# A convolution and retention trunk on one core: the rough mean goes into PSUM by ScalarE where the last four tiles begin, and the third weight pair is negated and added earlier

## The chip, the core and the metric
The kernel runs on one core of a Trainium2 chip. A core has five engines, each with a queue of its own that it works through in order: TensorE (PE: matrix products into PSUM), VectorE (DVE), ScalarE (ACT), GpSimd (POOL) and SyncE (SP, which only issues DMAs). PSUM is the small memory that TensorE writes; VectorE and ScalarE read and write it too, GpSimd does not. SBUF is the main memory on the core. The metric is device time in microseconds (us), the median over runs; less is better.

## The reference
Two layers on a sequence of 512 tokens with 1024 features: a causal convolution module and a retention module, each with a norm ahead, a gate and a residual, and one norm at the end. The change touches the first:

```python
def conv_module(h, w_in, dw_w, dw_b, ln_g, ln_b, w_out):
    proj = h @ w_in
    a, b, z = jnp.split(proj, 3, axis=-1)          # 2048 channels each
    u = a * jax.nn.sigmoid(b)
    c = causal depthwise convolution of u, 31 taps, + dw_b
    mu = jnp.mean(cf, axis=-1, keepdims=True)      # over the channels, for each token
    var = jnp.mean(jnp.square(cf - mu), axis=-1, keepdims=True)
    cn = (cf - mu) * lax.rsqrt(var + EPS) * ln_g + ln_b
    y = jax.nn.silu(cn) * jax.nn.silu(z)
    return y @ w_out
```

## The kernel before
Activations lie with channels on the 128 partitions and the 512 tokens along the free axis, so the 2048 channels of the convolution are 16 tiles `c_sb[0..15]` of 128x512. Matrix products run in float32 pieces: every operand is split into a rounded part (`hi`) and a rest (`lo`), and a product is three matmuls (`mm3`, lines 231 to 233): hi x hi, hi x lo, lo x hi.

Weights come from DRAM in 64 pairs of 1 MB (`load`, issued by SP) into two `raw` buffers. Pairs 3 to 23 are split like this: ScalarE writes minus the rounded weights to `lo` (`neg_hi`, line 196), a DMA issued by GpSimd adds `raw` onto it (`dma_lo`, line 204), and ScalarE writes the rounded weights to `hi` (`pos_hi`, line 200). A `raw` buffer is free for the pair after next when both its DMA and its positive copy have ended. Pairs 1 and 2 are split by ScalarE and GpSimd (`split_pair`) while the eight input tiles `h` are made (`h_tile`, `h_lo`).

TensorE works through units of 24 matmuls, two units to a pair; two units give one tile `u` (line 668, with a sigmoid by ScalarE, line 666), and units 32 to 47 give the gate (line 761). Beside that runs the convolution. Tile j is 31 multiplications of a shifted `u` by a column of `cpar`, added up. Two tiles are open at a time. VectorE does most taps (line 515), accumulating in one of two PSUM buffers (`ACC`). Other taps are products by ScalarE (line 434) that GpSimd adds up in SBUF (`accp`, line 442, which is `tadd`, line 297), or pairs of products (line 416) that a DMA issued by GpSimd adds (line 423). For tiles 2 to 11 ScalarE copies the sum of these into the PSUM buffer (`take_up`, line 467) and VectorE goes on from it. Tiles 0, 1 and 12 to 15 are `apart`: VectorE keeps its own sum in PSUM, and one add joins both parts at the end (line 494).

The variance needs the mean. After eight tiles TensorE has a rough mean (matmuls of line 642 and 653), which ScalarE puts into SBUF as `M0` (line 655). Tiles 0 to 11 have it subtracted by GpSimd (`shift`, line 596). In tiles 12 to 15 it is part of VectorE's first tap: `u * w - M0`, line 515 with `M0` as second tensor. Each finished, shifted tile is then summed over the channels by TensorE with a column of ones (`dsum`, line 286), squared by ScalarE (line 610), and the squares are summed, too (`st`). After all 16 sums the mean and variance are known and the layer goes on.

No scheduler orders this stage. The program keeps a clock of its own for each engine (`Clock`, costs written into the code), and at each step `fill` takes the piece of work that by these clocks can start first; what comes out is one fixed order for each engine, recorded as it is written. A change of a condition or of a step's place therefore changes the order of everything after it in this stage. Line numbers in the profile of the changed kernel are higher by up to 10.

## Time and profile before
| | us |
|---|---|
| median of 3 runs (lowest, highest) | 816.16 (814.44, 816.88) |
| the profiled execution | 812.21 |
| its span in the trace | 810.3 |
| TensorE busy | 786.7 (97%) |
| VectorE busy | 587.1 (72%) |
| ScalarE busy | 415.9 (51%) |
| GpSimd busy | 358.7 (44%) |

The busy shares are means over stages: in the convolution stage, from about 34 to 292 us, VectorE and TensorE are busy nearly all the time, and VectorE much less behind it. The profile names an instruction by line, engine and operation; `mm<-g,whi` writes a PSUM tile `mm` from the tiles `g` and `whi`, buffer numbers left out. Convolution tiles and `M0` are all called `g`; `acc` is a PSUM accumulator, `accp` a GpSimd sum, `u` an input of the convolution. What stands in square brackets is the idle time of that engine just before an instruction and what ended it. A timeline merges equal instructions that follow each other: `x5` with the time from the first's start to the last's end.

### The profile page before, as it was taken

Reading aid. Unit: us, or ns where it says so; the run is one execution under the profiler, and the core shown is the slowest. Engines: PE = TensorE matmul, PEld = TensorE weight load, DVE = VectorE, ACT = ScalarE, POOL = GpSimd, SP = SyncE. Lnnn points to the kernel's source line nnn. Section 1 sums busy time; section 2 is a strip of 40 time slices with the busy share of each in tenths; the row PEclk is TensorE's granted clock in tenths of the full one; section 3 lists DMA queues with packets and bytes.
Section 4 is the critical chain, followed back from the end, with each engine's and each line's share of the span. In section 5 each row is a group of like instructions: output and inputs, shape, how many; then the busy total and the mean of one; then the engine's idle time right before and its main releaser. Section 6 shows DMA issues by size and latency. Waiting matters only on the chain.

```text
span 810.3 us, 9659 instructions
## 1 busy us (share of the span) xinstructions
PE 786.7 (97%) x3649; PEld 648.6 (80%) x3650; DVE 587.1 (72%) x862; ACT 415.9 (51%) x550; POOL 358.7 (44%) x280
## 2 busy tenths in 40 slices
PE   7998999999999699999999999999999999999995
PEld 3586878888888587888888888888888888888895
DVE  4997999999999967899664657576586467552434
ACT  4588888878988636632433414414424524331421
POOL 0469999867999758740320223331340121000300
PEclk9999999999999889999999999999999999999999
DMA  7286767999789625422313212112112213323103
GB/s 273 105 208 158 199 169 177 216 217 228 202 195 244 185 47 182 182 97 106 110 53 104 77 79 104 53 53 104 53 53 105 104 53 104 104 91 116 53 1 104
DMA packets 19245, 102.61 MB, mean 127 GB/s; under 512 B 2304, under 2 KB 4352, under 8 KB 8320
## 3 DMA queue, kind: packets, MB, share of 16 engines
q1 hardware_dynamic: 14448, 74.73, 25.8%
q0 software_dynamic: 4320, 26.74, 16.9%
q10 hardware_dynamic: 432, 0.54, 0.2%
q8 instruction: 28, 0.46, 0.2%
q14 instruction: 17, 0.14, 0.1%
HBM read 73.17 MB, written 2.10 MB: 93 GB/s over the span
## 4 chain that ended last, share of the span: by engine, by line
PE 69%; DVE 12%; ACT 6%; POOL 4%; DMA 4%; issue 3%; DVEq 0%; POOLq 0%; ACTq 0%; SPq 0%
PE mm L231 20%; PE mm L232 20%; PE mm L233 20%; DVE acc L515 10%; POOL accp L297 4%; PE mm L958 2%; PE mm L957 2%; PE mm L956 2%; DMA wlo<-raw 1%; ACT wlo L196 1%; ACT whi L200 1%; ACT prod L434 1%; DMA raw<-wpack 1%; PE mm L326 1%; DMA g<-xT 1%
## 5 line engine op out<-in xcount | busy, mean ns | idle before, releaser
L231 PE MATMUL mm<-g,whi 128*128 128x512 f32 (+1 forms) x832 | 321.0, 386 | 0.0
L232 PE MATMUL mm<-g,whi 128*128 128x512 f32 (+1 forms) x832 | 318.5, 383 | 0.0
L233 PE MATMUL mm<-g,wlo 128*128 128x512 f32 (+1 forms) x832 | 317.7, 382 | 0.0
L515 DVE SCALAR_TENSOR_TENSOR acc<-u,cpar,acc 128x512 f32<-128x512 f32 x327 | 222.5, 750 | 6.8 <-ACT acc L467 5.5
L297 POOL TENSOR_TENSOR accp<-accp,prod 128x512 f32<-128x512 f32 x131 | 180.4, 1442 | 12.6 <-ACT prod L434 6.8
L231 PEld LDWEIGHTS mm<-g,whi 128*128 128x128 f32 x832 | 157.2, 189 | 30.9 <-issue 1.2
L232 PEld LDWEIGHTS mm<-g,whi 128*128 128x128 f32 x832 | 157.1, 189 | 30.3 <-issue 1.2
L233 PEld LDWEIGHTS mm<-g,wlo 128*128 128x128 f32 x832 | 157.0, 189 | 30.3 <-DMA wlo<-raw 0.2
L185 ACT CAST whi<-raw 128x1024 fp32r<-128x1024 f32 x80 | 80.6, 1050 | 111.4 <-PE mm L232 69.3
L190 DVE TENSOR_TENSOR wlo<-raw,whi 128x1024 fp32r<-128x1024 f32 x70 | 94.5, 1384 | 41.3 <-ACT whi L185 41.3
L297 POOL TENSOR_TENSOR g<-g,g 128x512 f32<-128x512 f32 x23 | 35.5, 1545 | 179.9 <-ACT g L293 171.4
L434 ACT ACTIVATE prod<-u,cpar 128x512 f32<-128x512 f32 x131 | 90.2, 717 | 24.9 <-POOL accp L297 24.8
L1044 POOL TENSOR_TENSOR g<-g,g 128x512 f32<-128x512 f32 x8 | 10.4, 1295 | 142.7 <-DVE g L1042 142.7
L226 DVE TENSOR_TENSOR g<-g,g 128x512 fp32r<-128x512 f32 x36 | 29.0, 820 | 35.7 <-ACT g L225 32.2
L225 ACT CAST g<-g 128x512 fp32r<-128x512 f32 x36 | 22.4, 621 | 60.1 <-POOL g L1044 27.8
L232 PE MATMUL mm<-wlo,g 128*128 128x512 f32 x128 | 49.8, 389 | 0.0
L233 PE MATMUL mm<-whi,g 128*128 128x512 f32 x128 | 49.6, 389 | 0.0
L231 PE MATMUL mm<-whi,g 128*128 128x512 f32 x128 | 49.3, 389 | 0.0
L196 ACT ACTIVATE wlo<-raw 128x2048 fp32r<-128x2048 f32 x21 | 40.1, 1909 | 4.5 <-DMA raw<-wpack 4.5
L200 ACT CAST whi<-raw 128x2048 fp32r<-128x2048 f32 x21 | 39.9, 1899 | 0.0
L1111 POOL TENSOR_TENSOR o<-o,g 128x512 f32<-128x512 f32 x16 | 27.5, 1748 | 18.2 <-DVE g L265 18.2
L204 POOL DMA_DIRECT2D wlo<-raw x21 | 20.0, 954 | 22.7 <-ACT wlo L196 18.7
(208 smaller groups left out, 971.4 us busy)
## 6 DMA issues: line engine op xcount, KB each, us to landing
raw<-wpack SPq DMA_DIRECT2D x63, 1024.0 KB, 4.8
wlo<-raw POOLq DMA_DIRECT2D x21, 1024.0 KB, 7.5
g<-xT SPq DMA_DIRECT2D x16, 256.0 KB, 6.2
q<-q POOLq DMA_DIRECT2D x6, 512.0 KB, 5.3
accp<-prod POOLq DMA_DIRECT2D x3, 512.0 KB, 4.6
out_dram<-xo SPq DMA_DIRECT2D x6, 256.0 KB, 2.3
dec<-decay SPq DMA_DIRECT2D x1, 1280.0 KB, 7.6
raw<-wpack ACTq DMA_DIRECT2D x2, 256.0 KB, 5.6
```

Of the source, the lines that this page charges most:

```text
L185: it.run(ACT_, 0.95, lambda: nc.scalar.copy(his[p][:, i, :], raws[p][:, i, :]), f"whi{n}")
L190: it.run(e, c, lambda: eng.tensor_tensor(out=lo, in0=raws[n // 2][:, n % 2, :], in1=hi.bitcast(F32), op=ALU.subtract), f"wlo{n}", [f"whi{n}"])
L196: it.run(ACT_, 1.8, lambda: nc.scalar.activation(los[p], raws[p], AF.Copy, scale=-1.0), f"wneg{p}")
L200: it.run(ACT_, 1.8, lambda: nc.scalar.copy(his[p], raws[p]), f"whi{p}", deps)
L226: (eng or nc.vector).tensor_tensor(out=lo, in0=src, in1=hi.bitcast(F32), op=ALU.subtract)
L231: nc.tensor.matmul(o, a[0], b[0], start=first, stop=False)
L232: nc.tensor.matmul(o, a[0], b[1], start=False, stop=False)
L233: nc.tensor.matmul(o, a[1], b[0], start=False, stop=last)
L297: eng.tensor_tensor(out=a, in0=a, in1=b, op=ALU.add)
L434: at = it.run(ACT_, 0.61, lambda: nc.scalar.activation(p, u_sb[j][:, w:w + S], AF.Copy, scale=cpar[:, j, w:w + 1]), at=add_end[n_prod[0]])
L515: it.run(DVE_, cost, lambda: nc.vector.scalar_tensor_tensor(out=c_sb[j] if last else acc, in0=u_sb[j][:, w:w + S], scalar=cpar[:, j, w:w + 1],
L1111: nc.gpsimd.tensor_tensor(out=t, in0=t, in1=RO, op=ALU.mult)
```

## The change
Where one of tiles 12 to 15 begins, ScalarE now writes minus `M0` into the PSUM accumulator (`take_up` has a branch for it), and VectorE's first tap adds to that accumulator like every other tap; the subtraction with `M0` from SBUF is gone. The planner counts such a tile as waiting for ScalarE (`WAITS`) until that is done. Apart from that, pair 3 is no longer split at the first full unit (n = 4): its negation and its adding DMA stand behind the eight `h` tiles, where the planner's clock of ScalarE is set to at least 31.5, and the loads of pairs 3 and 4 are called earlier; the positive copy stays at n = 4. What is computed is the same.

```diff
--- before.py
+++ after.py
@@ -446,7 +446,7 @@
         if apart(j):
             if not low[j]:
                 first_tap(j)
-            acc_ps[j] = (ACC(), stats["M0"], it.done["M0"]) if j > 1 else (ACC(), None, 0.0)
+            acc_ps[j] = (ACC(), WAITS, 0.0) if j > 1 else (ACC(), None, 0.0)
             high[j] = W
         else:
             if not low[j]:
@@ -464,6 +464,10 @@
     def take_up(j):
 
         acc = acc_ps[j][0]
+        if apart(j):
+            at = it.run(ACT_, 0.5, lambda: nc.scalar.activation(acc, stats["M0"], AF.Copy, scale=-1.0), deps=["M0"])
+            acc_ps[j] = (acc, acc, at + 0.1)
+            return
         at = it.run(ACT_, 0.5, lambda: nc.scalar.copy(acc, acc_sb[j]), at=acc_at[j])
         acc_ps[j] = (acc, acc, at + 0.1)
         release(j, at)
@@ -476,7 +480,7 @@
                 behind = max(behind, 5)
             return max(acc_at[j], it.now[POOL_] + 1.25 * behind if behind else 0.0)
         if acc_ps[j][1] is WAITS:
-            return max(acc_at[j], it.now[ACT_]) + 0.6
+            return max(it.done["M0"] if apart(j) else acc_at[j], it.now[ACT_]) + 0.6
         if acc_ps[j][1] is not None:
             return acc_ps[j][2]
         return 0.0
@@ -515,7 +519,7 @@
         it.run(DVE_, cost, lambda: nc.vector.scalar_tensor_tensor(
             out=c_sb[j] if last else acc, in0=u_sb[j][:, w:w + S], scalar=cpar[:, j, w:w + 1],
             in1=acc if start is None else start, op0=ALU.mult,
-            op1=ALU.add if start is None or not apart(j) else ALU.subtract),
+            op1=ALU.add),
             f"c{j}" if last else None, at=at if start is not None else 0.0)
         acc_ps[j] = (acc, None, 0.0)
         if last:
@@ -556,7 +560,7 @@
                     break
             for j in active:
                 if acc_ps[j][1] is WAITS:
-                    opts.append((max(it.now[ACT_], acc_at[j]), lambda j=j: take_up(j)))
+                    opts.append((max(it.now[ACT_], it.done["M0"] if apart(j) else acc_at[j]), lambda j=j: take_up(j)))
             if adds:
                 opts.append((max(it.now[POOL_], adds[0][2], acc_at[adds[0][0]]), pool_add))
             j = pool_tile() if len(adds) < PRODS else None
@@ -706,6 +710,7 @@
     h_tile(2)
     h_lo(1)
     list(pair)
+    load(3)
     pair = split_pair(2, 21.4)
     it.run(DVE_, 0.66, lambda: nc.vector.tensor_tensor(out=sg0, in0=pb, in1=R1_sb, op=ALU.mult), "bR", ["pab"])
     it.run(ACT_, 0.52, lambda: nc.scalar.activation(sg0, sg0, AF.Sigmoid), "sg", ["bR"])
@@ -727,6 +732,10 @@
     h_tile(7)
     h_lo(6)
     h_lo(7)
+    it.now[ACT_] = max(it.now[ACT_], 31.5)
+    neg_hi(3)
+    dma_lo(3)
+    load(4)
     ws = [unit(n) for n in (2, 3)]
     for k in range(KD):
         for c in range(2):
@@ -741,8 +750,6 @@
         for c in range(2):
             it.run(PE_, 0.227, lambda: nc.tensor.matmul(os_[c], ws[c][1][:, k * P:(k + 1) * P], h_s[k][0], start=False,
                                                        stop=k == KD - 1), f"mm{2 + c}", ["wlo1"])
-    load(3)
-    load(4)
 
     def unit_mm(n):
         o = MM()
@@ -775,11 +782,14 @@
             z_evict(n - 1, prev[0])
             prev = ()
         p = n // 2 + 1 + n % 2
-        if n == 4 or n % 2 and p < 24:
+        if n == 4:
+            pos_hi(3)
+            load(5)
+        elif n % 2 and p < 24:
             neg_hi(p)
             fill(it.done[f"wneg{p}"])
             dma_lo(p)
-        if n % 2 == 0:
+        if n > 4 and n % 2 == 0:
             pos_hi(p, [f"mm{n - 1}"])
             load(p + 2)
         prev = (prev or ()) + (unit_mm(n),)
```

The recorded order changes from ScalarE's 30th instruction on. Three places:

ScalarE behind the last `h` tiles, before (`wlo_376<-raw_353` is the negation of pair 3, `whi_385` its positive copy, `wlo_417` the negation of pair 4, `sg` the sigmoid for tile 1):
```order
L680 CAST g_298<-acc_300 128x512
L666 ACTIVATE sg_357<-mm_237 128x512
L434 ACTIVATE prod_369<-u_124,cpar 128x512
L434 ACTIVATE prod_373<-u_124,cpar 128x512
L196 ACTIVATE wlo_376<-raw_353 128x2048
L379 ACTIVATE accp_281<-u_125,cpar 128x512
L200 CAST whi_385<-raw_353 128x2048
L196 ACTIVATE wlo_417<-raw_355 128x2048
L434 ACTIVATE prod_449<-u_125,cpar 128x512
```
and with the change (`wlo_307`, `whi_379` and `wlo_422` are the same three):
```order
L684 CAST g_300<-acc_302 128x512
L196 ACTIVATE wlo_307<-raw_262 128x2048
L670 ACTIVATE sg_360<-mm_237 128x512
L434 ACTIVATE prod_372<-u_124,cpar 128x512
L434 ACTIVATE prod_376<-u_124,cpar 128x512
L200 CAST whi_379<-raw_262 128x2048
L379 ACTIVATE accp_283<-u_125,cpar 128x512
L434 ACTIVATE prod_415<-u_125,cpar 128x512
L434 ACTIVATE prod_419<-u_125,cpar 128x512
L196 ACTIVATE wlo_422<-raw_310 128x2048
L434 ACTIVATE prod_454<-u_125,cpar 128x512
```
The negation of pair 3 now stands ahead of the sigmoid, the positive copy one place earlier behind the products, and two products of tile 1 stand ahead of the negation of pair 4.

VectorE where tile 13 begins, before (`g_1611` is `M0`, `acc_2102` tile 13's accumulator, `acc_2001` tile 12's):
```order
L515 SCALAR_TENSOR_TENSOR g_1806<-u_125,cpar,acc_1805 128x512
L515 SCALAR_TENSOR_TENSOR acc_2001<-u_126,cpar,acc_2001 128x512
L515 SCALAR_TENSOR_TENSOR acc_2102<-u_127,cpar,g_1611 128x512
L515 SCALAR_TENSOR_TENSOR acc_2001<-u_126,cpar,acc_2001 128x512
L515 SCALAR_TENSOR_TENSOR acc_2102<-u_127,cpar,acc_2102 128x512
```
and with the change, the same place, and the place on ScalarE that goes with it (`acc_2097` is tile 13's accumulator, `g_1588` is `M0`, line 468 the new write):
```order
L519 SCALAR_TENSOR_TENSOR g_1880<-u_125,cpar,acc_1879 128x512
L519 SCALAR_TENSOR_TENSOR acc_1933<-u_126,cpar,acc_1933 128x512
L519 SCALAR_TENSOR_TENSOR acc_2097<-u_127,cpar,acc_2097 128x512
L519 SCALAR_TENSOR_TENSOR acc_1933<-u_126,cpar,acc_1933 128x512
L519 SCALAR_TENSOR_TENSOR acc_2097<-u_127,cpar,acc_2097 128x512
```
```order
L614 ACTIVATE q_2092<-g_1127 128x512
L614 ACTIVATE q_2092<-g_1274 128x512
L468 ACTIVATE acc_2097<-g_1588 128x512
L434 ACTIVATE prod_2101<-u_129,cpar 128x512
L768 ACTIVATE g_2105<-mm_2060 128x512
```
VectorE's instruction reads its own accumulator instead of `M0`; ScalarE has one instruction more, between two squares and a product.

GpSimd between the DMAs of pairs 15 and 16, before (`wlo_1531` and `wlo_1615`; line 649 is part of the rough mean):
```order
L297 TENSOR_TENSOR accp_1234<-accp_1234,prod_1526 128x512
L204 DMA wlo_1531<-raw_1390 128x2048
L649 TENSOR_TENSOR g_1282<-g_1279,g_1282 128x512
L204 DMA wlo_1615<-raw_1495 128x2048
L297 TENSOR_TENSOR accp_1429<-accp_1429,prod_1648 128x512
```
and with the change (`wlo_1544` and `wlo_1645`; line 600 is a shift):
```order
L653 TENSOR_TENSOR g_1291<-g_1274,g_1291 128x512
L204 DMA wlo_1544<-raw_1400 128x2048
L297 TENSOR_TENSOR accp_1483<-accp_1483,prod_1537 128x512
L297 TENSOR_TENSOR accp_1483<-accp_1483,prod_1541 128x512
L297 TENSOR_TENSOR accp_1483<-accp_1483,prod_1576 128x512
L297 TENSOR_TENSOR accp_1483<-accp_1483,prod_1583 128x512
L297 TENSOR_TENSOR accp_1483<-accp_1483,prod_1599 128x512
L297 TENSOR_TENSOR accp_1483<-accp_1483,prod_1602 128x512
L297 TENSOR_TENSOR accp_1483<-accp_1483,prod_1638 128x512
L600 TENSOR_TENSOR g_363<-g_363,g_1588 128x512
L204 DMA wlo_1645<-raw_1502 128x2048
```
One instruction stood between the two DMAs, and now eight do. In all, GpSimd has 142 adds of products where it had 131, and the three pair DMAs of line 423 are gone; ScalarE has 142 products of line 434 for 131, none of line 416 for 6, and 4 writes more; VectorE has 336 taps of line 515 for 341. TensorE has the same instructions; the sum of tile 12 stands 72 matmuls ahead of that of tile 13, where it stood 24 ahead. The sum of tile 15 is three matmuls behind that of tile 14. SP's order is the same, and so is every engine's order behind the sums.

## Rows read from the trace of the kernel before

**Rows 1.** The page's part 1: busy us, share of the span, instructions.
```profile
PE 786.7 (97%) x3649; PEld 648.6 (80%) x3650; DVE 587.1 (72%) x862; ACT 415.9 (51%) x550; POOL 358.7 (44%) x280
```

**Rows 2.** TensorE's waits, whole span: us in total, times, longest us.
```profile
PE dsum L286 <- DVE g L494: 6.5, 2, 6.0
PE st L642 <- DVE g L494: 2.7, 1, 2.7
```

**Rows 3.** Timeline of TensorE, 262 to 300: start, us, instruction [idle before].
```profile
268.01 1.05 PE L286 MATMUL dsum<-ones,g 128*128 128x1 f32 x8 [0.49 <-DVE g L494]
...
274.28 0.39 PE L233 MATMUL mm<-g,wlo 128*128 128x512 f32 x1
280.65 1.87 PE L286 MATMUL dsum<-ones,g 128*128 128x1 f32 x8 [5.98 <-DVE g L494]
...
290.49 0.95 PE L286 MATMUL dsum<-ones,g 128*128 128x1 f32 x8
```

**Rows 4.** Windows: busy us by engine (instructions), granted clock, DMA share, GB/s.
```profile
40.00:290.00 250.00, 240.79 (x1059) 197.16 (x1058) 241.21 (x354) 204.20 (x247) 214.11 (x176) 0.98 0.79 196
...
281.00:292.00 11.00, 11.00 (x43) 9.22 (x43) 10.75 (x17) 5.47 (x9) 8.65 (x7) 0.69 0.25 48
```

**Rows 5.** Timeline of VectorE in the last tiles.
```profile
236.63 3.09 DVE L515 SCALAR_TENSOR_TENSOR acc<-u,cpar,g 128x512 f32<-128x512 f32 x1
...
267.28 0.68 DVE L494 TENSOR_TENSOR g<-accp,acc 128x512 f32<-128x512 f32 x1
...
268.54 4.89 DVE L515 SCALAR_TENSOR_TENSOR acc<-u,cpar,g 128x512 f32<-128x512 f32 x1
...
279.92 0.67 DVE L494 TENSOR_TENSOR g<-accp,acc 128x512 f32<-128x512 f32 x1
...
281.18 0.75 DVE L515 SCALAR_TENSOR_TENSOR acc<-u,cpar,g 128x512 f32<-128x512 f32 x1
...
291.72 0.69 DVE L494 TENSOR_TENSOR g<-accp,acc 128x512 f32<-128x512 f32 x1
```

**Rows 6.** Timeline of GpSimd, seven places: its gaps and its adds.
```profile
40.00 2.68 POOL L297 TENSOR_TENSOR accp<-accp,prod 128x512 f32<-128x512 f32 x2 [6.83 <-ACT prod L434]
...
46.96 0.87 POOL L204 DMA_DIRECT2D wlo<-raw  x1 [3.30 <-ACT wlo L196]
...
60.73 0.88 POOL L204 DMA_DIRECT2D wlo<-raw  x1 [3.43 <-PE mm L233]
...
149.56 0.88 POOL L204 DMA_DIRECT2D wlo<-raw  x1 [2.48 <-ACT wlo L196]
...
184.92 0.88 POOL L204 DMA_DIRECT2D wlo<-raw  x1 [7.70 <-ACT wlo L196]
...
268.48 7.45 POOL L297 TENSOR_TENSOR accp<-accp,prod 128x512 f32<-128x512 f32 x5
...
281.56 0.88 POOL L619 DMA_DIRECT2D q<-q  x1 [5.63 <-ACT q L610]
282.17 8.43 POOL L297 TENSOR_TENSOR accp<-accp,prod 128x512 f32<-128x512 f32 x6
```

**Rows 7.** VectorE's waits, 33 to 295.
```profile
DVE acc L515 <- ACT acc L467: 5.5, 6, 1.9
DVE u L668 <- ACT sg L666: 2.4, 1, 2.4
```

**Rows 8.** Timeline of ScalarE, three places.
```profile
38.71 0.60 ACT L666 ACTIVATE sg<-mm 128x512 f32<-128x512 f32 x1 [5.57 <-PE mm L742]
...
58.51 1.92 ACT L196 ACTIVATE wlo<-raw 128x2048 fp32r<-128x2048 f32 x1 [2.85 <-DMA raw<-wpack]
...
75.18 0.59 ACT L467 COPY acc<-accp 128x512 f32<-128x512 f32 x1 [0.65 <-POOL accp L297]
```

**Rows 9.** Weight loads issued from 25 to 60: issue ns, first and last start, landing.
```profile
L166 SPq DMA_DIRECT2D raw<-wpack x4: 327/328/328, 27.5 to 56.3; - x4
...
DMA to landing us min/median/max: 4.8/5.6/8.7
```


## The prediction
> **What bounds the kernel now.** I read the page's busy times first, then TensorE's waits, then the stretch behind its longest wait engine by engine, and last the earlier places where VectorE falls back. TensorE is busy 786.7 us of a span of 810.3 [rows 1], and its list of waits names little outside the convolution stage, so the change is worth what it takes out of TensorE's waits in that stage. Two matter: 6.5 us for token sums of finished tiles (`dsum`), 6.0 of them in one piece, and 2.7 us for one mean matmul (`st`, line 642) [rows 2]. Both wait for a VectorE add of line 494, the last step of a tile.
>
> The long one: the last matmul ahead of it starts at 274.28, the sum of tile 13 at 280.65 [rows 3]. It costs more than its 5.98 us. From the sum of tile 12 (268.01) to 274.28 + 0.23, one sum and 24 matmuls took 6.50; from the sum of tile 13 to that of tile 14 (280.65 to 290.49) the same work took 9.84 [rows 3]. The granted clock from 281 to 292 is 0.69 [rows 4]: TensorE came out of the idle time at the lower of its two levels. So 3.34 us more hang on this wait. With 0.49 before tile 12's sum and 2.7 at line 642, TensorE can get back 5.98 + 3.34 + 0.49 + 2.7 = 12.5 us.
>
> Why is tile 13 late? VectorE is not idle there; it has two long instructions. Starting tile 13 took 3.09 us and starting tile 14 4.89, where the same instruction for tile 15 took 0.75 [rows 5]. They read the rough mean (`g`) from SBUF beside `u`, also in SBUF. While the second was held, GpSimd ran adds in SBUF back to back (five from 268.48 to 275.93); when tile 15 began at 281.18, GpSimd was in a gap of 5.63 us, with no add running [rows 5, 6]. Over the 0.75 they cost 2.34 and 4.14, together 6.48 us.
>
> VectorE is also behind from earlier: it waits 2.4 us for `sg` and up to 1.9 for an accumulator that ScalarE copies [rows 7]. The root is ScalarE's wait of 2.85 us at 58.51 for a weight load [rows 8]: everything behind it in ScalarE's queue slips.
>
> **The change part by part.**
>
> *Third pair earlier.* ScalarE is idle for 5.57 us before 38.71, so from 33.14; the negation (1.92 us) now stands there [rows 8]. Its load is issued at 27.5 and such loads land after 4.8 to 8.7 us, 5.6 at the median [rows 9]: at 33.1, at the worst 36.2, and the negation ends at 35 to 38.1, before the sigmoid at 38.71 either way. The accumulating DMA goes out behind it, in GpSimd's gap of 6.83 us before 40.00 [rows 6], instead of between adds. SP issues the same loads in the same order. The load that ScalarE waited for arrived at 58.5, so it was issued at 49.8 or later (8.7 at most); it waits for the pair's raw buffer. That is now free when the positive copy ends, behind the sigmoid and two products, near 42.5: some 7 us earlier against a wait of 2.85. The wait goes, and with it VectorE's 2.4 and 1.9. If the cover fails, these 4.3 us stay.
>
> *Mean into PSUM.* The first tap of tiles 12 to 15 now has one operand in PSUM, like the other taps, whose mean from start to start is 0.65 (from tile 12's add to tile 13's: 12.64 us less 4.14, for 13 instructions [rows 5]). The 6.48 us go. ScalarE gets four writes; the copy at 75.18, 0.59 us, is the nearest row [rows 8]. What VectorE waits for them is bounded by 0 and the 1.9 of the longest such wait before; I take 0 for the sum, since two tiles are always open and the other one's taps run meanwhile, and price the rest as a rival.
>
> The Trainium skill (SBUF — State Buffer, "Who interferes with whom") says that a VectorE instruction with two SBUF inputs and a GpSimd one that reads SBUF exclude each other, the second waiting until the first has finished. One add takes about 1.3 us, so by this rule 2.6 of the 6.48 us are explained and 3.9 have another cause and stay; the trace shows VectorE held through two and three adds in a row. By the rule alone tile 12's sum would wait 0.4, tile 13's 0.7 and tile 15's 1.7 us, a gain of 9.7, or 806.5; I go by the trace.
>
> *What the recorded order makes of it.* The three pair products by DMA (lines 416, 423) are gone; 11 more products go through ScalarE and GpSimd's adds, and VectorE has 5 taps less. Counted in VectorE's order, the closing adds of tiles 12, 13, 14 and 15 stand 12, 2, 7 and 5 places earlier, that of tile 1 seven places. With the times of [rows 3, 5]:
> - Line 642: tile 1's add is 7 x 0.65 = 4.6 us earlier by its place alone, more than the 2.7 waited. Gone.
> - Tile 12: 267.28 - 7.9 (12 places) - 2.4 - 1.9 - 2.34 = 252.7, done 253.4. Tile 13's sum can start at 268.01 - 0.49 - 2.7 + 6.50 = 271.3. Tile 12's now stands 72 matmuls ahead of it, 17.3 us with its own time: 254.0. No wait, by 0.6.
> - Tile 13: 279.92 - 1.3 - 6.6 - 4.14 = 267.9, done 268.5, for 271.3. No wait, by 2.8.
> - Tile 15: 291.72 - 3.3 - 10.8 = 277.6, done 278.3. Its sum now follows tile 14's after three matmuls: 271.3 + 6.5 + 1.6 = 279.4. No wait by VectorE alone.
>
> But tile 15's closing add also waits for GpSimd. Before, its last add ends at 282.17 + 8.43 = 290.6 [rows 6]. Gaps that go: 3.43 (that load), 5.63 (tile 13 late), and 3.30, 2.48 and 7.70, where adds now stand ahead of the DMA that ended the gap: 22.5. Added: 11 x 1.40 (six in 8.43) = 15.4. Issues gone from this stretch: four of 0.88, of which 0.6 at least count: 2.4 to 3.5. Together 280.0 to 281.1; in the middle, with 0.6 for the closing add, tile 15 is done at 281.1, and TensorE waits 1.7 us. GpSimd is busy 214 of 250 us before [rows 4]; (214 + 15 - 3) of 240 is 94%, and it is what this stage's end now waits for.
>
> Sum: 12.5 - 1.7 = 10.8 us. The profiled execution took 812.2 (1.9 more than its span) and would take 801.4; the median of the runs is 816.16, 4 us more for the same program, so **the forecast is 805.4 us**. Behind the stage all engines keep their order.
>
> **Rivals.**
> - *Late accumulators.* A start that needed nothing of ScalarE now waits for its queue. Before there are 6 such waits, 5.5 us in all, the longest 1.9 [rows 7]. At 0.9 each: 1.2 us at tile 12's sum, 1.3 at tile 15's, gain 10. At 1.95 each: 3.3 and 3.4, gain 5.8, 810.4. For it: GpSimd, on which ScalarE's products wait, gets fuller. Against: only four places.
> - *The hold is not due to the operand.* Then 6.48 us of VectorE stay: waits of 1.7 at tile 12, 2.0 at 13, 1.7 at 15; gain 7.1, 809.1. Against: 0.75 at tile 15, with GpSimd not adding.
> - *GpSimd too late: slower.* In the gaps of 3.30, 2.48 and 7.70 GpSimd waits for ScalarE's negations [rows 6]; an add there needs a product, ScalarE's too. If these 13.5 us stay, the last add ends at 294.0, tile 15 at 294.6, and TensorE waits 15.2 us at its sum and loses 3.3 to the low clock: 12.5 - 18.5 = -6.0, 822.2. It decides from a last add at 288.
> - *All covered:* 12.5 us, 803.7.
>
> **How the numbers follow.** The forecast with a gain of 9 to 12.5 (803.7 to 807.2) 0.63; late accumulators at more than 0.9 each 0.14; hold stays 0.11; GpSimd late by part of its gaps but still faster 0.04, slower 0.04; no effect on the end 0.04. Runs of this kernel tell about 0.3%, 2.4 us. Faster by more: 0.63 + 0.14 + 0.11 + 0.04 = 0.92; same 0.04; slower 0.04. The range goes from 802.5 (full gain, and the 1.2 us by which the runs differ) to 810.5, the dear end of the first rival, which holds the second; 0.1 lies above it, 0.05 below. The unknown price, four writes at 0 to 1.95, is inside.
>
> **What will show it.** Right: no tap of VectorE over 0.8 us; ScalarE's third negation at 33, and no wait for a load near 58; no wait of TensorE at the second mean matmul; granted clock 1.00 near 280; GpSimd's last add near 280. Wrong: a wait of TensorE over 3 us at any `dsum`: at tile 12's for want of an accumulator, at tile 15's for want of GpSimd.

## The result, and the profile after

The changed kernel took 817.8 us (median of 20 runs, 815.73 to 821.18), the kernel before on the same chip 813.87 (20 runs, 807.76 to 817.64): a ratio of 1.0051 [1.0034, 1.0067]. It is slower by half a per cent; forecast was 805.4, a ratio of 805.4 / 816.16 = 0.9868. The profiled execution took 816.26 us with a span of 814.5 (before: 812.21 and 810.3).

The first view is a table of windows of the changed kernel: busy us of TensorE, its weight loads, VectorE, ScalarE and GpSimd, then granted clock, DMA share and GB/s.

```profile
40.00:204.00 164.00, 164.00 (x715) 133.99 (x714) 160.46 (x243) 144.07 (x173) 153.89 (x125) 1.00 0.71 183
204.00:300.00 96.00, 88.81 (x403) 75.12 (x403) 72.94 (x111) 66.33 (x88) 72.25 (x60) 0.90 0.73 178
```

Up to 204 us TensorE has no gap at all (164.00 of 164). Before, the same window looked like this:

```profile
40.00:204.00 164.00, 161.25 (x702) 131.28 (x701) 156.65 (x237) 136.82 (x162) 136.19 (x112) 1.00 0.79 196
```

The difference is the wait at line 642 [rows 2], which is gone: TensorE is 13 matmuls further on (x715 for x702). All of the loss lies behind 204. TensorE's waits after:

```profile
PE dsum L286 <- POOL g L600: 4.5, 1, 4.5
PE dsum L286 <- DVE g L498: 2.7, 1, 2.7
```

They answer to the 6.5 and 2.7 of [rows 2]: 7.2 us in place of 9.2, so the idle time has even become less. On TensorE's timeline:

```profile
251.74 1.87 PE L286 MATMUL dsum<-ones,g 128*128 128x1 f32 x8 [4.50 <-POOL g L600]
...
260.39 0.94 PE L286 MATMUL dsum<-ones,g 128*128 128x1 f32 x8
277.67 0.95 PE L286 MATMUL dsum<-ones,g 128*128 128x1 f32 x8
284.06 0.95 PE L286 MATMUL dsum<-ones,g 128*128 128x1 f32 x8
288.51 1.87 PE L286 MATMUL dsum<-ones,g 128*128 128x1 f32 x8 [2.69 <-DVE g L498]
291.66 1.70 PE L286 MATMUL st<-ones,q 128*128 128x1 f32 x8
```

These are the sums of tiles 11 to 15 (one mean matmul behind them). Those of tiles 12, 13 and 14 wait for nothing, but tile 11's waits 4.5 us for GpSimd's subtraction of the mean, and tile 15's 2.69. Behind each the sum takes 1.87 us in place of 0.95: TensorE runs at the lower of its two levels. The windows show it:

```profile
249.00:257.00 8.00, 5.26 (x18) 4.56 (x19) 8.00 (x13) 4.61 (x7) 6.36 (x6) 0.57 0.97 215
...
288.00:304.00 16.00, 15.49 (x60) 14.37 (x61) 3.52 (x17) 1.76 (x3) 0.85 (x2) 0.50 0.13 34
```

At 0.50, one sum and three matmuls take 291.66 - 288.51 = 3.15 us; before, tile 14's sum and the three behind it took 1.59 (290.49 [rows 3] to 292.08). Between 40 and 310 us the clock's own record has low stretches of 6.8 us from 249.6 and 17.1 us from 287.1; before it had one of 10.2 us at 277.5. So from 288.51 to 304.04 about 7.8 of 15.5 us are lost to the clock, and some 2.3 of 4.7 behind 251.74: 4.5 + 2.7 + 7.8 + 2.3 = 17.3 us against the 12.5 counted for before. The first matmul of the next stage starts at 312.53 in place of 308.65, 3.9 us later, and the spans differ by 4.2.

What made the sums late? ScalarE's waits, 40 to 310 us, after:

```profile
ACT q L614 <- DMA q<-q: 10.5, 3, 4.6
ACT q L614 <- DVE g L498: 2.7, 1, 2.7
```

The first stood at 1.4 us in all before:

```profile
ACT q L610 <- DMA q<-q: 1.4, 2, 1.2
```

Line 614 squares a centred tile into `q`; two squares fill that one buffer, line 623 adds it to the running sum by an accumulating DMA of 0.5 MB, and the next pair waits until the DMA has landed. The queue of ScalarE is served in order, so all behind the square waits too:

```profile
205.50 1.32 ACT L434 ACTIVATE prod<-u,cpar 128x512 f32<-128x512 f32 x2
211.42 0.63 ACT L614 ACTIVATE q<-g 128x512 f32<-128x512 f32 x1 [4.60 <-DMA q<-q]
211.96 0.58 ACT L471 COPY acc<-accp 128x512 f32<-128x512 f32 x1
...
242.93 0.63 ACT L614 ACTIVATE q<-g 128x512 f32<-128x512 f32 x1 [3.46 <-DMA q<-q]
243.47 0.58 ACT L768 ACTIVATE g<-mm 128x512 f32<-128x512 f32 x1
243.95 1.91 ACT L196 ACTIVATE wlo<-raw 128x2048 fp32r<-128x2048 f32 x1
...
256.09 1.15 ACT L614 ACTIVATE q<-g 128x512 f32<-128x512 f32 x2 [2.42 <-DMA q<-q]
...
261.88 0.58 ACT L468 ACTIVATE acc<-g 128x512 f32<-128x512 f32 x1
```

The first of these three waits ends when a DMA has landed that GpSimd issued at 201.30; below it the landing times of all DMAs of line 623:

```profile
201.30 0.87 POOL L623 DMA_DIRECT2D q<-q  x1
```

```profile
DMA to landing us min/median/max: 4.5/6.6/10.0
```

GpSimd and VectorE stand behind those instructions (two timelines):

```profile
246.15 0.87 POOL L204 DMA_DIRECT2D wlo<-raw  x1 [3.72 <-ACT wlo L196]
...
249.81 1.87 POOL L600 TENSOR_TENSOR g<-g,g 128x512 f32<-128x512 f32 x1
```

```profile
212.57 0.75 DVE L519 SCALAR_TENSOR_TENSOR acc<-u,cpar,acc 128x512 f32<-128x512 f32 x1 [5.70 <-ACT acc L471]
...
262.49 13.93 DVE L519 SCALAR_TENSOR_TENSOR acc<-u,cpar,acc 128x512 f32<-128x512 f32 x21 [4.62 <-ACT acc L468]
...
287.77 0.69 DVE L498 TENSOR_TENSOR g<-accp,acc 128x512 f32<-128x512 f32 x1
```

The chain of tile 11: the DMA issued at 233.98 lands, the square starts at 242.93, the negation behind it at 243.95, GpSimd's weight DMA at 246.15, the subtraction at 249.81, TensorE's sum at 251.74. VectorE loses 5.70 us behind the square of 211.42, whose own wait was 4.60. It loses 4.62 more for the write of tile 13's mean (line 468, 261.88); of these the square ahead of it, at 256.09, explains 2.42 at most. VectorE's last closing add ends at 288.5, where the prediction had 281.1 (278.3 by VectorE alone).

### The profile page after: what moved, and what is told of

Its sections match the earlier page's. It is cut to its first block, busy times and chain, and to the rows that moved or that the text cites. A ratio compares the mean times of both kernels' runs of the same rounds, so it can differ in the third digit from the quotient of the medians.

```text
span 814.5 us, 9679 instructions
## 1 busy us (share of the span) xinstructions
PE 794.9 (98%) x3649; PEld 656.4 (81%) x3650; DVE 577.7 (71%) x857; ACT 420.5 (52%) x559; POOL 368.7 (45%) x288
## 4 chain that ended last, share of the span: by engine, by line
PE 89%; DMA 3%; DVE 3%; POOL 2%; ACT 2%; issue 1%; ACTq 0%; DVEq 0%; POOLq 0%
PE mm L231 26%; PE mm L232 25%; PE mm L233 25%; DMA q<-q 2%; POOL accp L297 2%; PE mm L326 2%; PE mm L968 2%; PE mm L966 2%; PE mm L967 2%; PE st L286 1%; DVE acc L519 1%; PE acc L233 1%; PE acc L232 1%; PE acc L231 1%; DMA raw<-wpack 1%
## 5 line engine op out<-in xcount | busy, mean ns | idle before, releaser
L297 POOL TENSOR_TENSOR accp<-accp,prod 128x512 f32<-128x512 f32 x142 | 192.1, 1385 | 19.5 <-ACT prod L434 13.1
L434 ACT ACTIVATE prod<-u,cpar 128x512 f32<-128x512 f32 x142 | 97.5, 716 | 23.9 <-POOL accp L297 23.7
L1054 POOL TENSOR_TENSOR g<-g,g 128x512 f32<-128x512 f32 x8 | 10.3, 1294 | 142.6 <-DVE g L1052 142.6
L190 POOL TENSOR_TENSOR wlo<-raw,whi 128x1024 fp32r<-128x1024 f32 x10 | 24.1, 2411 | 9.3 <-ACT whi L185 9.3
```

The lines of the kernel that those rows point to most:

```text
L190: it.run(e, c, lambda: eng.tensor_tensor(out=lo, in0=raws[n // 2][:, n % 2, :], in1=hi.bitcast(F32), op=ALU.subtract), f"wlo{n}", [f"whi{n}"])
L297: eng.tensor_tensor(out=a, in0=a, in1=b, op=ALU.add)
L434: at = it.run(ACT_, 0.61, lambda: nc.scalar.activation(p, u_sb[j][:, w:w + S], AF.Copy, scale=cpar[:, j, w:w + 1]), at=add_end[n_prod[0]])
```

## The experiments

Theory Q: the new order puts the squares too close behind the landing of the previous pair, and ScalarE's queue carries that wait to all engines. Rival G: the DMA engines and GpSimd are full from 195 us on, and some wait arises whatever is done. Rival P: one of the two edits is worth nothing or costs time. Rival A: ScalarE's four writes of the mean come late and are the price. Theory C came in with the low stretches: most of what is left is the clock behind a short wait, not the wait.

**e1: two square buffers, the same order.** No instruction moves on any engine.

```diff
-            stats["q"] = cp.tile([P, 2, S], F32, tag={0: "qsum", KI - 2: "prod2"}.get(i, "q"), bufs=1, name=nm("q"))
+            stats["q"] = cp.tile([P, 2, S], F32, tag="q" if i // 2 % 2 else "prod2" if i else "qsum", bufs=1, name=nm("q"))
```

> The changed kernel with the same order on every engine; the pairs of squares take turns in two buffers (the second is the one that pair products used, now unused). Theory Q (ScalarE's queue is held by squares that wait for the accumulating DMA of the pair before, 10.5 us in three waits, and VectorE's starts of tiles 11 and 14 and TensorE's sums wait behind it): ScalarE's waits for q fall under 2 us, VectorE's waits for lines 468 and 471 from 14.0 to under 5, TensorE's dsum waits from 7.2 to under 3, granted clock near 1.00 in 249 to 257, and the time 9 to 12 us under the kernel before, ratio 0.985 to 0.989. Rival G (GpSimd is full and sets the end, the waits for q are only where it shows): GpSimd's last add stays near 287 and the time within 2 us of the changed kernel, ratio 1.003 to 1.007. Rival A (the four writes by ScalarE are the price): VectorE's waits for line 468 stay near 5.7 and the gain on the changed kernel is under 3 us.

811.59 us, ratio 0.9976 [0.9955, 0.9998]. The q waits (ScalarE's for the `q` buffer) are gone, and with them 0.75% of the time against the changed kernel's 1.0051. That part belongs to the buffer. It is less than theory Q expected (0.985 to 0.989), so more than the squares is at work. G may have a part, which no run isolates: a weight load now comes late. Half of what rival A named is there, too: VectorE still waits 5.8 and 1.2 us for writes of the mean, though the gain is more than the 3 us that A allowed. Tile 15's sum still waits 2.70:

```profile
240.44 1.92 ACT L196 ACTIVATE wlo<-raw 128x2048 fp32r<-128x2048 f32 x1 [4.43 <-DMA raw<-wpack]
```

```profile
284.47 1.86 PE L286 MATMUL dsum<-ones,g 128*128 128x1 f32 x8 [2.70 <-DVE g L498]
...
287.62 1.70 PE L286 MATMUL st<-ones,q 128*128 128x1 f32 x8
```

From 284.4 the clock is low for 17.1 us, as it was after.

**e3 and e4: each edit alone, order written anew for it.** e3 leaves out the moves of the third pair, e4 leaves the mean in SBUF (excerpts).

```diff
 e3 (against the changed kernel)
-    load(3)
...
-    neg_hi(3)
-    dma_lo(3)
-    load(4)
...
 e4 (against the changed kernel)
-            acc_ps[j] = (ACC(), WAITS, 0.0) if j > 1 else (ACC(), None, 0.0)
+            acc_ps[j] = (ACC(), stats["M0"], it.done["M0"]) if j > 1 else (ACC(), None, 0.0)
...
```

> The kernel before with only the mean put into PSUM by ScalarE; the third pair stays where it was, and the order keeps the three pair products. Theory Q: the two held instructions (6.48 us) go, the 2.85 us wait for a load stays, and squares still wait some 2 to 3 us each at two or three places because the order places them 3 to 5 us behind the DMA; ratio 0.990 to 0.997. Rival A (the writes are the price): VectorE waits 5 us or more for line 468 and the time is not under the kernel before, ratio 1.000 or more. Rival G: ratio near 0.99 or below, since this order has no more adds than before.

> The kernel before with only the third pair earlier; the mean is still read from SBUF. Theory Q: the wait for the load at 58 us goes, but the order that follows has no pair products, squares 3 to 7 us behind the DMA as in the changed kernel, and VectorE's long instructions stay: q waits of 7 us or more, ratio 1.003 to 1.012, as slow as the changed kernel or slower. My prediction's reading (moving the pair only helps): ratio 0.990 to 0.996. Rival G: ratio 1.003 or more with GpSimd's last add the latest thing before TensorE's last sum.

e3: 814.73, ratio 1.0015 [0.9999, 1.0031]. e4: 816.87, 1.0042 [1.0022, 1.0061]. Neither alone gains, and in both orders ScalarE is held by the q buffer, 6.9 us in four waits in e3 and 10.8 in four in e4. So the squares' waits do not come from one of the edits; they come with a newly written order. e3 also has what rival A named, one wait of 6.2 us of VectorE for a write of the mean and a time not under before; a square that waited 2.92 us at 267.36 stands ahead of that write (271.31) in ScalarE's queue and explains a part of it. e4, with the mean in SBUF, has a VectorE hold again:

```profile
237.88 7.01 DVE L515 SCALAR_TENSOR_TENSOR acc<-u,cpar,g 128x512 f32<-128x512 f32 x1
```

**e5: the order of before, only the operand in PSUM.** ScalarE's write is put in where tiles 12 to 15 begin, and nothing else is planned anew (excerpt).

```diff
+            if j > 1:
+                nc.scalar.activation(acc_ps[j][0], stats["M0"], AF.Copy, scale=-1.0)
+                acc_ps[j] = (acc_ps[j][0], acc_ps[j][0], it.done["M0"])
```

> The kernel before with its own order on every engine and only this in it: at the start of tiles 12 to 15 ScalarE writes minus the mean into the accumulator and VectorE adds to that. Isolates the operand. If two SBUF operands beside GpSimd's adds are the cause of the 3.09 and 4.89 us instructions, all first taps take 0.75, tile 13's sum comes 4 to 6 us earlier, and the ratio is 0.989 to 0.994. If the hold has another cause, the long instructions stay and the ratio is 0.998 to 1.003. If the four writes come late (rival A), VectorE waits for them 4 us or more and the ratio is about 0.998 as well, but with short instructions.

809.27, ratio 0.9955 [0.9931, 0.9979]. The edit is worth something where the order stays. No tap is long, ScalarE's q wait is 1.7 us, and the four writes cost VectorE 2.2 us in two waits, between the 0 taken and the bound of 1.9 each:

```profile
DVE acc L518 <- ACT acc L451: 2.2, 2, 1.2
```

**e9: both edits in the order of before** (excerpt).

```diff
 (e5, and in the h tiles:)
+    nc.scalar.activation(los[3], raws[3], AF.Copy, scale=-1.0)
+    nc.gpsimd.dma_start(out=los[3], in_=raws[3], accum_op=ALU.add)
```

> The order of before kept on every engine (nothing re-planned), with both edits laid on it: the mean goes to PSUM for the writes of the last four tiles, and the third pair is loaded, negated and added during the h tiles. Theory Q with the order (both edits are worth their part, the loss came from the new order that they brought about): the gain of the PSUM mean in the old order (ratio 0.9955) plus the 2.85 us ScalarE wait at 58 us, of which VectorE's and GpSimd's later slack may keep part: 804 to 808 us (ratio 0.988 to 0.994). Rival (the third pair's move has itself no worth or costs): 809 to 813 us (0.995 to 1.000).

810.35, ratio 0.9940 [0.9911, 0.9970]: at the edge between the two expectations, and not to be told from e5. Whether the third pair has a worth of its own in this order stays open. Its gap went (TensorE is busy all 164 us from 40 to 204), but the profile has 3.8 us of waits and 13.7 us at the low clock near the end.

**e6: the changed kernel, with longer DMA durations in its order.** The program that writes the order counts on fixed durations for the DMAs. I set them near the time that their packets take in the traces: 1 MB weight adds 5.2 us, 0.5 MB adds 2.7, loads 3.5. (For the loads that is too much: from 190 to 262 us after the change their packets took 3.0 us each. And all are short of the time to landing, which for the 0.5 MB adds of the squares is 4.5 us and more.)

```diff
-            it.land(2.92, ...)                 # loads
+            it.land(3.5, ...)
-        it.done[f"wlo{p}"] = it.land(2.92, at + 0.4)
+        it.done[f"wlo{p}"] = it.land(5.2, at + 0.4)
-        end = it.land(1.46, at)
+        end = it.land(2.7, at)
-        q_free[0] = it.land(1.46, at)
+        q_free[0] = it.land(2.7, at)
```

> The changed kernel; only the durations by which its recorded order counts on the accumulating DMAs are set to what the traces show (1 MB weight adds 5.2 us, 0.5 MB adds of square pairs and product pairs 2.7 us, loads 3.5 us). The order is written anew from these, so steps move. Theory Q (ScalarE is held by the next pair of squares until the DMA that adds the previous pair has landed; the new order put the squares too close behind): the squares move later, the four waits of 2.4 to 4.6 us on the q buffer fall to about 1 us each, the 4.5 us TensorE wait near 250 us goes with its low clock, 811 to 813 us (ratio 0.995 to 0.999). Rival G (DMA engines and GpSimd are simply full between 195 and 256 us, whoever waits): the waits only move to other steps, 815 to 819 us (ratio 1.000 to 1.006).

803.37, ratio 0.9877 [0.9848, 0.9905]: close to the gain that was forecast for the change (0.9868), and more than theory Q expected of this run. No square waits for the buffer; the one behind the first DMA (issued at 200.29) now comes 16.9 us later, where the changed kernel had it 5.5 us behind the issue (201.30, and ScalarE free at 206.82):

```profile
198.94 0.62 ACT L614 ACTIVATE q<-g 128x512 f32<-128x512 f32 x1
...
217.14 0.62 ACT L614 ACTIVATE q<-g 128x512 f32<-128x512 f32 x1
```

The DMAs themselves got no faster: 4.6, 6.7 and 10.3 us from issue to landing (least, median, most), after the change 4.5, 6.6 and 10.0. TensorE's waits from 40 us to the end of the stage:

```profile
PE mm L233 <- DMA wlo<-raw: 1.4, 1, 1.4
PE dsum L286 <- DVE g L498: 0.8, 1, 0.8
```

**e11 and e12: which duration.** e11 sets only the 0.5 MB adds to 2.7, e12 only the weight adds and loads (two lines each of the diff above).

> The changed kernel with only the 0.5 MB adds (square pairs, product pairs) set to 2.7 us in its recorded order. Theory Q (it was the squares put too close behind the landing of the pair before): the q waits fall from 10.5 to under 4 us in all and the time comes near e6's, 803 to 808 us (ratio 0.988 to 0.994). Rival W (the weight adds' true duration, which shifts loads and GpSimd's steps, was what counted): 813 to 818 us (ratio 1.000 to 1.006).

> The changed kernel with only the 1 MB weight adds (5.2 us) and loads (3.5 us) set to their measured durations in its recorded order, the 0.5 MB adds left as they were. Theory Q: the q waits stay near 10 us in all, 814 to 819 us (ratio 1.000 to 1.007). Rival W: the waits go and the time is near e6's, 803 to 808 us (ratio 0.988 to 0.994).

e11: 806.19, ratio 0.9929 [0.9907, 0.9952], in the range that theory Q gave; but the q waits fell only to 4.5 us in one wait, more than expected. e12: 812.65, 1.0011 [0.9988, 1.0034]: no gain over before, yet its q waits fell too, to 1.2, which speaks against the simple form of theory Q. Neither expectation holds for e12: the waits went, the time did not come. The square behind the first DMA comes 16.9 us behind it in e12 as in e6 (201.83, 218.69), and still waits 4.5 us in e11; so the weight durations moved it, not the squares' own. The two profiles show where the time went. e11, timeline of TensorE:

```profile
274.31 1.87 PE L286 MATMUL dsum<-ones,g 128*128 128x1 f32 x8 [4.24 <-DVE g L498]
283.96 0.95 PE L286 MATMUL dsum<-ones,g 128*128 128x1 f32 x8
```

and e12:

```profile
284.00 1.87 PE L286 MATMUL dsum<-ones,g 128*128 128x1 f32 x8 [2.63 <-DVE g L498]
287.15 1.70 PE L286 MATMUL st<-ones,q 128*128 128x1 f32 x8
290.14 1.70 PE L286 MATMUL st<-ones,q 128*128 128x1 f32 x8
293.13 3.41 PE L286 MATMUL st<-ones,q 128*128 128x1 f32 x16
```

Both waited about as long in all (4.2 us; 2.6 and 1.5 for a weight). In e11 the wait came ahead of a long run of split matmuls, and the clock was low for 6.8 us; in e12 ahead of the closing sums, which have only three matmuls between them, and it was low for 17.1. The next stage began at 302.13 and 308.66. The orders differ in more than this, so the place of the wait is a likely reason and not a shown one.

**e7: e1, with 13 matmuls that nobody reads ahead of tile 15's sum.** About 0.22 us each (the row below shows 12 of the 13).

```diff
+        for _ in range(13 if which and n_sum[1] == KI - A else 0):
+            nc.tensor.matmul(idle, wz[:, 0:P], wz, start=True, stop=True)
```

> The kernel with two square buffers (e1) plus 13 matmuls of 128x512 into an unused bank (about 0.22 us each at the high clock, results unused) ahead of the last tile's sum over partitions, where TensorE otherwise idles 2.7 + 1.7 us and then ran 17.1 us at the 1.2 GHz level. Theory C (most of what is left of the loss is the clock after a short idle, not the idle itself): the 17.1 us stretch goes or shrinks to under 7 us, the first out-projection matmul starts 5 to 8 us earlier than e1's 309.1, 804 to 807 us (ratio 0.989 to 0.993). Rival (the clock falls whatever fills the gap, or the matmuls just add their own 2.8 us): 811 to 814 us (0.998 to 1.002).

805.82, ratio 0.9914 [0.9881, 0.9946], against e1's 0.9976. Theory C holds for this wait:

```profile
285.31 2.75 PE L633 MATMUL mm<-wz 128*128 128x512 bf16 x12
287.89 0.95 PE L286 MATMUL dsum<-ones,g 128*128 128x1 f32 x8
...
289.48 0.95 PE L286 MATMUL st<-ones,q 128*128 128x1 f32 x8
```

The sum comes 3.4 us later than in e1, but it and the three matmuls behind it take 1.59 us in place of 3.15. Of the 17.1 us at the low level 3.4 stay (from 294.5). Another 6.8 us stand at 274.0, where e1 had none; they and a wait of 2.0 us at 273.78 come ahead of the idle matmuls, where both kernels are the same, and make tile 14's sum 3.5 us later. One profile can differ from the next by that much. The profiled gain to the next stage is 3.0 us (306.10 for 309.12), less than the 5 to 8 expected; the medians differ by 5.8.

**e8: two square buffers known to the order, durations of e6** (excerpt).

```diff
-        q_free[0] = it.land(1.46, at)
+        q_land.append(it.land(2.7, at))
+        q_free[0] = q_land[-2]
```

> The changed kernel with two square buffers that the recorded order knows of, and its DMA durations set to those of the traces. Theory Q: no squares wait, and with the order planned for it the closing adds of tiles 13 and 15 come at about 271 and 281 us, 807 to 810 us (ratio 0.992 to 0.996). Rival G (DMA engines full from 195 to 256 us): a weight load or add lands late instead, as pair 21's did with two buffers alone (4.4 us), 811 to 814 us (0.998 to 1.001).

808.13, ratio 0.9936 [0.9906, 0.9966]: in theory Q's range, but no better than e6. No square waits for a buffer, TensorE waits 1.9 us in all, but the clock is low for 6.8 us at 237.6 and 10.2 at 288.8. The second stretch has no wait ahead of it; two windows of e8:

```profile
284.00:292.00 8.00, 8.00 (x45) 6.99 (x44) 3.03 (x6) 3.30 (x5) 2.37 (x1) 0.80 0.31 82
292.00:300.00 8.00, 8.00 (x34) 7.34 (x34) 3.60 (x14) 0.00 (x0) 1.52 (x2) 0.56 0.01 2
```

TensorE is busy 8.00 of 8.00 us in both, with the closing sums. So theory C, the clock behind a short wait, does not cover every low stretch.

**e10 and e13: controls for e6.** e10 is the kernel before with the durations of e6; e13 is e3 with them (PSUM mean, third pair as before).

> The kernel before, without either edit; only the durations by which its recorded order counts on the accumulating DMAs and loads are set to those of the traces, as in e6, and the order is written anew. It is the control for e6 (ratio 0.9877). Theory R (the gain of e6 belongs to the two edits, which needed an order that knows the DMAs): before had only 1.4 us of waits on the q buffer, so little to gain: 810 to 814 us (ratio 0.997 to 1.002). Rival N (the better durations alone are the gain, the edits are worth nothing): 803 to 806 us (ratio 0.988 to 0.992).

> Only the mean in PSUM (third pair as in before), with the measured DMA durations of e6 in its recorded order: splits e6's gain. If theory R holds and the held-back VectorE instructions (6.48 us) are the larger part, 806 to 809 us (ratio 0.991 to 0.995), and the third pair is worth the 3 to 5 us that are left to e6. Rival: the third pair is worth nothing here (ScalarE's 2.85 us wait is taken up later by its own slack), 802 to 805 us (0.986 to 0.990).

e10: 827.42, ratio 1.0179 [1.0131, 1.0226]. The better durations alone are no gain (rival N falls), and the kernel before fares much worse by them than theory R had it. What stands out is one instruction on VectorE:

```profile
234.90 21.41 DVE L515 SCALAR_TENSOR_TENSOR acc<-u,cpar,g 128x512 f32<-128x512 f32 x1
```

It is a first tap that reads the mean from SBUF, the kind that took 3.09 and 4.89 in before [rows 5]. GpSimd adds in SBUF without a gap from 233.99 to 255.74, with three DMA issues in between; two of its rows of e10:

```profile
237.74 4.09 POOL L297 TENSOR_TENSOR accp<-accp,prod 128x512 f32<-128x512 f32 x3
...
247.68 5.91 POOL L297 TENSOR_TENSOR accp<-accp,prod 128x512 f32<-128x512 f32 x4
```

TensorE then waited 5.38 and 9.26 us for sums. e13: 810.49, ratio 0.9976 [0.9955, 0.9998], above both expectations. GpSimd's sequence in that stretch is the same to within 1.5 us, and VectorE, with the mean in PSUM, runs 42 taps of 0.66 us:

```profile
233.53 27.85 DVE L519 SCALAR_TENSOR_TENSOR acc<-u,cpar,acc 128x512 f32<-128x512 f32 x42
```

So with these durations the PSUM mean is worth 17 us (827.42 to 810.49). e6, which has the third pair earlier as well, is 7 us faster still (810.49 to 803.37), but the order differs between these two kernels, and e13's clock is low for 17.1 us at 285.8 where e6's is for 6.8.

**All runs in one table.** Waits: those of TensorE from 40 to 310 us at sums, means and split matmuls. Low: us at the low level from 230 us to the start of the next stage, from the clock's record in the trace. Start: first matmul of the next stage. The ratio is of medians; the other columns are of the one profiled execution, which can lie off the median (e7's took 809.55 us, its median is 805.82).

```
          ratio   waits   low  start
before    1       9.2    10.2  308.65
after     1.0051  7.2    23.9  312.53
e1        0.9976  4.4    20.5  309.12
e3        1.0015  8.8    17.1  311.09
e4        1.0042  7.0    17.1  311.73
e5        0.9955  5.4     3.4  304.59
e6        0.9877  2.1     6.8  300.07
e7        0.9914  2.3    10.2  306.10
e8        0.9936  1.9    17.1  307.27
e9        0.9940  3.8    13.7  307.76
e10       1.0179 15.9    30.7  325.62
e11       0.9929  4.2     6.8  302.13
e12       1.0011  4.2    17.1  308.66
e13       0.9976  2.4    17.1  308.43
```

Start less waits less half of low lies between 293.4 and 297.5 in every row (of e7 also less the 2.6 us of its idle matmuls), while the starts spread over 25.6 us. So waits and half of the low time say most of what an order is worth; the 4 us that are left are as much as lies between many of the rows, and are not explained.

## Why the prediction was wrong

*What bounds the kernel:* right, and the two wait lines were those to remove. Of the 12.5 us to get back, e6, which has the change's two edits, got 8.6: it starts the next stage at 300.07 in place of 308.65.

*Third pair earlier:* right for its own stretch. The negation starts at 31.80 and ScalarE is idle behind it until 38.78; the load wait near 58 is gone; VectorE's 2.4 us wait became 0.3. The wait at line 642 went with it.

*Mean into PSUM:* right for the long instructions. No tap is over 0.8 us. The rival that the operand was not the cause falls by e5, e10 and e13. The writes, though, I took at 0 with a bound of 1.9, and that bound was too low in nearly every newly written order: 4.62 and 1.12 us after, at most 5.8 in e1, 6.2 in e3, 4.7 in e8, 4.6 in e12 and 2.0 in e13; only e11 has 0.4. In e6 it is still 4.3, and there TensorE's sums wait no more than 0.8; in the order of before (e5) it is 1.2.

*The rule of the Trainium skill (SBUF — State Buffer, "Who interferes with whom"):* the prediction weighed whether one GpSimd add is all that a VectorE instruction with two SBUF inputs is held by. The trace went against that: 7.01 us in e4 and 21.41 in e10, through many adds. But adds alone do not decide it. The start of tile 12 in before, which the prediction passed over, likewise read `u` and the mean from SBUF and took 0.75 us while GpSimd ran three adds in a row:

```profile
226.75 0.75 DVE L515 SCALAR_TENSOR_TENSOR acc<-u,cpar,g 128x512 f32<-128x512 f32 x1
```

```profile
225.64 4.27 POOL L297 TENSOR_TENSOR accp<-accp,prod 128x512 f32<-128x512 f32 x3
```

What lets one such instruction through and holds the next is open.

*What the recorded order makes of it: this step failed.* It moved tiles forward by their places in VectorE's order and by GpSimd's gaps and adds. It took for granted that "tile 15 is done at 281.1" needs VectorE and GpSimd alone, and did not walk down ScalarE's new order. There ScalarE reaches the next pair's square 5.5 us behind the issue of the DMA that frees the buffer (201.30 to 206.82; the other two 5.5 and 5.7), and that DMA lands after 4.5 to 10 us; before, the first pair had 12.7 us (214.84 to 227.59). The landing times were a view of before that I read only for the loads [rows 9]. Tile 15's add ended at 288.5, 10.2 us later than VectorE's own reckoning of 278.3, and tile 11's sum, which I had not priced at all, waited 4.5 us. e1, with every instruction in its place, shows the buffer's part: tile 15's add ends at 284.4, 4.0 us earlier, and 0.75% comes back. The other 6.1 us are as much as VectorE's waits for the writes of the mean in e1 (5.80 and 1.23): VectorE is ready for tile 13 at 252.5, and ScalarE's queue has a step of the gate, the negation of a pair and two products ahead of the write at 257.73. That, too, stands in ScalarE's new order.

*The clock: put at nothing.* The sum left TensorE a wait of 1.7 us at tile 15's sum and no low clock behind it. Only the slower rival had 3.3 us for it, from the one case in before, a wait with 24 matmuls behind it. Ahead of the closing sums a 2.69 us wait was followed by a stretch that cost about 7.8 us more. In all, 7.2 us of waits and 10.1 us of clock stand where the sum had 1.7 and 0. In e7 the idle matmuls bring the low time behind tile 15's sum from 17.1 to 3.4 us, and another 0.62% comes back. So e1 and e7, in the changed kernel's own order, account for 1.37 of the 1.83 per cent between forecast (0.9868) and result (1.0051).

*The rivals.* "GpSimd too late" had the right sign and the wrong mechanism: its last add ended at 283.55 + 2.92 = 286.5, below the 288 from which it was to decide, and its late gaps were ScalarE's waits in another guise (behind the square of 211.42 it waited 2.22 and 2.83 us for products, behind that of 242.93 3.72 for a negation). "Late accumulators" named the right line for VectorE's 4.62 us, at more than twice its dear end, and is a part of the lateness. No rival named the squares, and none the clock by itself.

What stays open: what brings e6 from e1's 0.9976 to 0.9877. No square waits in either, many steps moved, and no run isolates one. The squares' waits alone do not set the time: they are 0 in e1, e10 and e13, too, and e12 has 1.2 us of them and gained nothing over before. The third pair's own worth is not settled either: nothing to be seen in e9 against e5, about 1% in e6 against e13, where the orders differ.

## What to carry to other kernels

When an order is written anew, walk down the queue of every in-order engine, not only of those that were late: look for the buffer with a single copy and compare, in the new order, the distance from the DMA that frees it to its next writer with the landing times of the trace. Durations in a planner matter where an order relies on them, but longer ones are no remedy by themselves: the same four numbers turned the change's loss into nearly the forecast gain (e6) and cost the kernel before 1.8% (e10). And price a wait of TensorE with the clock behind it, by the place where it stands: the low stretch was 17.1 us ahead of the closing sums (2.7 us waited in e1, 2.6 in e12) and 6.8 ahead of a long run of matmuls (4.2 us waited in e11).

## What the runs showed of the hardware

A single VectorE instruction of 0.75 us with both tensors in SBUF stood for 21.41 us while GpSimd ran adds in SBUF back to back (e10), and 42 taps with one operand in PSUM ran at 0.66 us each beside the same adds (e13). The DMA issues that GpSimd had in between (242.74, 244.56 and 253.20 in e10) did not release it. The same kind of instruction took 0.75 us beside adds at 226.75 in before.

An accumulating DMA of 0.5 MB from SBUF to SBUF, 4.5 us from issue to landing at its quickest, took 10.0 when a 1 MB load was issued 0.05 us behind it (201.30 and 201.35 after) and a 1 MB add at 205.19. With two square buffers (e1) the landings were longer still, 4.6, 8.5 and 13.2 us (least, median, most); why is not shown.

Low stretches of the clock came behind waits as short as 0.77 us (e6, at 282.24; low for 6.8 us from 284.5), and in e8 without one: with TensorE busy 8.00 of 8.00 us in the closing sums the granted clock was 0.80, then 0.56. In before, tile 14's sum and the sums behind it ran at the high level (0.95 us from 290.49 [rows 3]).
